# Sixteen of a hybrid decoder layer's 24 gate blocks as pairs of seven half-size products, behind the gMLP units

## The chip, the core and the metric

The kernel runs on one core of a Trainium2 chip. The core has a matrix engine (PE), a vector engine (DVE), a scalar engine (ACT), GpSimd (POOL), a sync engine (SP) that here only issues loads, on-chip memory (SBUF), accumulation banks (PSUM) and DMA queues to DRAM. Each engine works through its own list of instructions in order; semaphores hold an instruction until what it needs is done. The metric is the device time in microseconds (us), the median of three runs. The profile is a trace of one execution.

## The reference

One layer over 1024 tokens of 1024 channels. The normed rows feed one input projection; three mixers (A gMLP, B RG-LRU, C SSD) work on parts of it. Each mixer's output goes through a branch matrix and is weighted by a sigmoid gate that is itself a 1024-column block of the projection. A feed-forward part follows.

```python
hn = rms_norm(h, norm_mix_g[l])
proj = jnp.einsum('bsd,de->bse', hn, w_in[l])
za, zb, zc, xbc, dt_raw, g_raw = jnp.split(proj, SPLIT_POINTS, axis=-1)
ya = gmlp_mixer(za, ...); yb = rg_lru_mixer(zb, ...); yc = ssd_mixer(zc, xbc, dt_raw, ...)
gates = jax.nn.sigmoid(g_raw.reshape(bsz, seq, N_BRANCHES, D_MODEL) + b_gate[l])
merged = (gates[:, :, 0] * jnp.einsum('bse,ed->bsd', ya, w_branch_a[l])
          + gates[:, :, 1] * jnp.einsum('bse,ed->bsd', yb, w_branch_b[l])
          + gates[:, :, 2] * jnp.einsum('bse,ed->bsd', yc, w_branch_c[l]))
h = h + jnp.einsum('bsd,de->bse', merged, w_out[l])
hn = rms_norm(h, norm_mlp_g[l])
up = jax.nn.relu(jnp.einsum('bsd,df->bsf', hn, w_mlp_up[l]))
h = h + jnp.einsum('bsf,fd->bsd', up * up, w_mlp_down[l])
```

## The kernel before

**Tiling.** Channels lie on the 128 partitions, tokens along the row. A float32 operand is split into a rounded high part (ACT, L131) and the rest as a low part (DVE, or POOL for every third weight, L132). A product of two split operands takes three matmuls: high by high, high by low, low by high. A *unit* is 128 output columns of a projection for all 1024 tokens: 8 slices of the inner dimension times 3 parts times 2 token halves, 48 matmuls of 128x512 into one PSUM tile `ps` (`product`, L492 to L498). `run` (L500) takes units from a queue. It first brings the weights of the next units in (`wtile`: load into one of two `raw` buffers, split into the six-buffer pool `w`), then multiplies, then runs the unit's `post`, then `step`, which advances every pending generator by one stage. The compiler's scheduler then sets the order on each engine; code inside `tc.manual_schedule()` keeps the order in which it is written.

**Stages.** First come the norm and the V blocks of gMLP. Then four *rounds* follow (L817 to L823). In each, `ssd_units` queues six units, `lru_units` two units per head for two heads, and gate units of branches 1 and 0 stand between and behind them: one after the SSD units, one after the first head, two after the second (none in the last round). The stages of a mixer (`ssd_stages`: `s1_` to `s4_` for two token halves; `stages` of `lru_units`) run beside later units. Stage `s4_` begins with a matmul of ones by a sum of squares (L683); that sum is a POOL addition (L678) of two squares by ACT (L677) of what `s3_` makes last on DVE (L675). Behind the rounds come the eight gMLP units, each with a Gelu of two ACT and two DVE operations in `post` and a mixing of 16 small matmuls (L788) one unit later, with the last two gate units of branch 0; then the eight gate units of branch 2, whose results stay in SBUF (`keep_gate`), with the rows of `yc` loaded and split beside them (`load_next`, L873, through the two `raw` buffers); then 24 branch units, c, b and a, each of which multiplies its product by (1 + tanh) of the gate (L881 to L885). Then come the output projection (L914 to L945; its PSUM banks come free when x rows loaded on ACT's queue, L938, are added), and the feed-forward part.

**The seven-product scheme** already stands in the feed-forward part: a 2x2 block product with seven half-size products (Strassen's, in Winograd's form) instead of eight. `Weights` (L1007) loads two column blocks and makes the sums of quarters S1 to S4; `seventh` (L958) is one such product, 12 matmuls of 128x512; `Super` (L1050) runs p1 to p7 of it.

**Pools.** `act` has 15 tiles of 128x1024 and ends, with `half`, `lruw` and `const`, before the branches, where `act2` with 27 tiles opens. `mainps` holds two `ps` tiles, `auxps` four half-size tiles.

Of the kernel before, what the change touches and what calls it, by code (L numbers as in the profile page):

```python
# [16 lines left out]
P = 128  # L17
# [19 lines left out]
def trunk_kernel(ctx: ExitStack, tc: tile.TileContext, x, norm_mix_g, w_in, b_gate, gmlp_ln_g, gmlp_ln_b,  # L37
# [20 lines left out]
    xp = normed.enter_context(tc.tile_pool(name="xn", bufs=16, side="right"))  # L58
    mixers = ExitStack()
    halfp = mixers.enter_context(tc.tile_pool(name="half", bufs=16))  # L60
    pools = [mixers.enter_context(tc.tile_pool(name="act", bufs=15))]
# [401 lines left out]

    def wtile(src, n=[0]):
# [55 lines left out]
    gd = [dram.tile([KD, P, T], F32, name=f"g{b}_d") for b in range(2)]  # L520
# [259 lines left out]
    def gmlp_unit(g):  # L780
        def stages(u2):
            yield
# [19 lines left out]
    def gate_unit(br, e, kept=None):  # L802
        def post(ps):
            t = act()
            actv(t, ps, AF.Tanh, scale=0.5, bias=vh[:, BG + br * 8 + e:BG + br * 8 + e + 1])
            if kept:
                kept(t)
            else:
                nc.gpsimd.dma_start(out=gd[br][e], in_=t)
        unit_in(C_G + br * D + e * P, post)  # L810

    gates = [(br, e) for br in (1, 0) for e in range(8)]
# [31 lines left out]
    merged = []  # L844

    def keep_gate(t):
        merged.append(t)
        for k in range(2 * len(merged) - 2, min(2 * len(merged), KD)):
            load_next("c", k)

    for e in range(KD):
        gate_unit(2, e, keep_gate)
    ahead(AHEAD)
    mixers.close()
    pools[0] = ctx.enter_context(tc.tile_pool(name="act2", bufs=27, reuse_waits="tile"))
    late = []

    def act3(shape=(P, T), dt=F32):
        return late[0].tile(list(shape), dt, tag="act3", name=nm("b"))


    def load_y(b, k):
        raw = rawp.tile([P, T], F32, tag="raw", name=nm("raw"))
        nc.sync.dma_start(out=raw, in_=yd[b][k])
        new = act3 if b == "b" else act
# [12 lines left out]
    def branch_unit(b, br, w, e, nxt):  # L878
        def post(ps):
            if b == "c":  # L880
                stt(out=merged[e], in0=merged[e], scalar=1.0, in1=ps, op0=ALU.add, op1=ALU.mult)  # L881
            else:
                t = act()
                nc.scalar.dma_start(out=t, in_=gd[br][e])
                stt(out=t, in0=t, scalar=1.0, in1=ps, op0=ALU.add, op1=ALU.mult)  # L885
# [13 lines left out]
    run()  # L899
    normed.close()  # L900
    late.append(ctx.enter_context(tc.tile_pool(name="act3", bufs=16, side="right", reuse_waits="tile")))
# [44 lines left out]

    sub = ALU.subtract  # L950

    def w4(shape=(P, T), dt=F32):
        return wp.tile(list(shape), dt, tag="w", name=nm("wt"))

    def r4(shape=(P, T), dt=F32):
        return rawp.tile(list(shape), dt, tag="raw", name=nm("rt"))

    def seventh(ps, lhs, rhs, new):  # L958

        n = 0  # L960
        for kk in range(4):
            for l, r in ((0, 0), (0, 1), (1, 0)):
                mm(ps, lhs[l][kk], rhs[r][kk], start=(new and n == 0), stop=(n == 11), skip_group_check=not new)  # L963
                n += 1
# [41 lines left out]

    class Weights:  # L1007


        def __init__(self, src, col, new):  # L1010
            self.new = new
            self.a, self.b = r4((P, KD, P)), act((P, KD, P))
            for t, c0 in ((self.a, col), (self.b, col + P)):
                nc.sync.dma_start(out=t, in_=src[:, c0:c0 + P].rearrange("(k p) e -> p k e", p=P))
            self.op = {}

        def both(self, names, t):
            hi, lo = self.new((P, KD, P), F32R), self.new((P, KD, P), F32R)
            split(hi, lo, t)
            for i, n in enumerate(names):  # L1020
                self.op[n] = [[p[:, 4 * i + kk, :] for kk in range(4)] for p in (hi, lo)]

        def cast1(self):
            self.both(("A11", "A12"), self.a)

        def sums1(self):
            self.s12, self.s34 = act((P, KD, P)), act((P, KD, P))
            tt(out=self.s12[:, 0:4], in0=self.b[:, 0:4], in1=self.b[:, 4:8], op=ALU.add)
            tt(out=self.s34[:, 0:4], in0=self.a[:, 0:4], in1=self.b[:, 0:4], op=sub)

        def sums2(self):
            tt(out=self.s12[:, 4:8], in0=self.s12[:, 0:4], in1=self.a[:, 0:4], op=sub)
            tt(out=self.s34[:, 4:8], in0=self.a[:, 4:8], in1=self.s12[:, 4:8], op=sub)

        def cast12(self):
            self.both(("S1", "S2"), self.s12)

        def cast34(self):
            self.both(("S3", "S4"), self.s34)

        def cast22(self):
            t = act((P, KD, P), F32R)
            split(t[:, 0:4], t[:, 4:8], self.b[:, 4:8])
# [416 lines left out]
```

## Time and profile before

| what | value |
|---|---|
| median of three runs (2030.2 to 2032.55) | 2030.78 us |
| time of the profiled execution | 2033.04 us |
| span of its trace | 2031.3 us |
| mean granted PE clock | 0.991 |
| the four rounds | 127.5 to about 815 us |
| gMLP units, the last two gates of branch 0, the gates of branch 2 | about 815 to 1026 us |
| branch units | to 1287 us |
| output projection, feed-forward part | 1287 to 2031 us |

How to read it: a view of groups gives, for one line of the kernel, engine and shape, how many instructions there were, their busy time and the mean length of one, and what the engine waited for ahead of them. A timeline row is start, length, engine, line, operation, output <- inputs; in brackets stands how long the engine was idle just before and what ended that. A table of windows gives each engine's busy time in a stretch, the granted PE clock (1.00 is full speed), the DMA share and GB/s. PE rows overlap, since matmuls are pipelined; the distance of starts is what one costs.

### The profile page before, as it was taken

The numbers are of one execution on the slowest core, as the hardware profiler recorded it, in microseconds if no ns is written. First come the engines' busy times: TensorE is split into PE (matmuls) and PEld (weight loads), VectorE is DVE, ScalarE is ACT, GpSimd is POOL, SyncE is SP. The second block draws the span as 40 slices with busy tenths as digits, with TensorE's granted clock in tenths as the row PEclk, the third lists the DMA queues.
The fourth block names the chain that finished last, engine by engine and source line by source line (L and its number), as shares of the span: only waits on it lengthen the run. The fifth ranks groups of instructions, "written<-read, shape, count | busy, mean of one in ns | idle before, by whom it ended". The sixth has DMA issues, their size and how long they took to land.

```text
span 2031.3 us, 23733 instructions
## 1 busy us (share of the span) xinstructions
PE 1985.2 (98%) x9300; PEld 1658.2 (82%) x9300; DVE 1196.5 (59%) x1819; ACT 788.4 (39%) x1081; POOL 348.7 (17%) x362
## 2 busy tenths in 40 slices
PE   7999999999999999999999999999899999999996
PEld 7998888888888888888888888887688887888885
DVE  5597774684677468532123224436756657787787
ACT  6422452354245225422221212246555555243243
POOL 4012141222124213431000320000111111000000
PEclk9999999999999999999999999999999999999998
DMA  4224322522422433433333442421444448644532
GB/s 156 76 105 86 89 82 68 113 76 83 96 76 85 95 86 73 127 122 104 114 104 106 148 133 82 165 83 63 155 149 147 161 140 302 211 131 138 187 107 91
DMA packets 202212, 239.38 MB, mean 118 GB/s; under 512 B 11140, under 2 KB 148564, under 8 KB 202100
## 3 DMA queue, kind: packets, MB, share of 16 engines
q1 hardware_dynamic: 175636, 144.91, 24.1%
q0 software_dynamic: 21680, 75.64, 11.6%
q10 hardware_dynamic: 4784, 17.31, 2.4%
q8 instruction: 73, 1.20, 0.3%
q14 instruction: 39, 0.32, 0.1%
HBM read 174.78 MB, written 63.05 MB: 117 GB/s over the span
## 4 chain that ended last, share of the span: by engine, by line
PE 87%; DVE 5%; ACT 4%; issue 2%; POOL 1%; ACTq 0%; POOLq 0%; DVEq 0%
PE ps L497 49%; PE aux L963 26%; PE aux L256 4%; PE aux L932 3%; PE aux L748 1%; ACT a L992 1%; PE aux L788 1%; PE aux L645 1%; DVE rsq_q L110 1%; PE aux L665 1%; PE aux L669 1%; PE aux L683 0%; ACT a L131 0%; DVE b L132 0%; ACT a L970 0%
## 5 line engine op out<-in xcount | busy, mean ns | idle before, releaser
L497 PE MATMUL ps<-xn,wh 128*128 128x512 f32 x2304 | 624.5, 392 | 0.0
L497 PEld LDWEIGHTS ps<-xn,wh 128*128 128x128 f32 x2304 | 430.9, 188 | 93.0 <-issue 4.5
L497 PE MATMUL ps<-xn,wl 128*128 128x512 f32 x1152 | 354.9, 389 | 0.0
L131 ACT ACTIVATE wh<-raw 128x1024 fp32r<-128x1024 f32 x96 | 101.6, 1059 | 394.5 <-PE ps L497 321.2
L497 PEld LDWEIGHTS ps<-xn,wl 128*128 128x128 f32 x1152 | 216.2, 188 | 45.2
L963 PE MATMUL aux<-a,b 128*128 128x512 f32 x864 | 197.3, 389 | 0.0
L963 PEld LDWEIGHTS aux<-a,b 128*128 128x128 f32 x864 | 162.2, 188 | 33.6
L132 DVE TENSOR_TENSOR wl<-raw,wh 128x1024 fp32r<-128x1024 f32 x64 | 81.4, 1271 | 180.9 <-ACT wh L131 179.0
L132 POOL TENSOR_TENSOR wl<-raw,wh 128x1024 fp32r<-128x1024 f32 x32 | 76.8, 2401 | 547.5 <-ACT wh L131 520.9
L963 PE MATMUL aux<-b,wt 128*128 128x512 f32 x672 | 156.9, 389 | 0.0
L963 PEld LDWEIGHTS aux<-b,wt 128*128 128x128 f32 x672 | 126.1, 188 | 26.2
L497 PE MATMUL ps<-a,wh 128*128 128x512 f32 x512 | 136.8, 389 | 0.0
L497 PEld LDWEIGHTS ps<-a,wh 128*128 128x128 f32 x512 | 96.1, 188 | 20.0
L963 PE MATMUL aux<-b,b 128*128 128x512 f32 x480 | 110.6, 389 | 0.0
L1212 DVE TENSOR_TENSOR a<-aux,a 128x512 f32<-128x512 f32 x112 | 76.9, 687 | 50.5 <-PE aux L963 50.5
L963 PEld LDWEIGHTS aux<-b,b 128*128 128x128 f32 x480 | 90.1, 188 | 18.7
L131 ACT ACTIVATE b<-wt 128x1024 fp32r<-128x1024 f32 x60 | 61.9, 1054 | 70.2 <-DMA wt<-u_d 63.9
L963 PE MATMUL aux<-a,wt 128*128 128x512 f32 x336 | 80.3, 396 | 3.4 <-ACT a L1089 3.4
L497 PE MATMUL ps<-a,wl 128*128 128x512 f32 x256 | 78.8, 389 | 0.0
L963 PEld LDWEIGHTS aux<-a,wt 128*128 128x128 f32 x336 | 64.1, 191 | 17.7 <-ACT a L1089 4.2
L517 DVE SCALAR_TENSOR_TENSOR a<-ps,scw,a 128x1023 f32<-128x1023 f32 (+2 forms) x48 | 61.4, 1279 | 25.5 <-ACT a L515 24.5
L1064 POOL DMA_DIRECT2D u_d<-a x48 | 34.6, 721 | 226.2 <-DVE a L1112 177.5
(296 smaller groups left out, 2949.9 us busy)
## 6 DMA issues: line engine op xcount, KB each, us to landing
raw<-in_w_in_dram SPq DMA_DIRECT2D x72, 512.0 KB
wt<-u_d SPq DMA_DIRECT2D x54, 512.0 KB
u_d<-a POOLq DMA_DIRECT2D x48, 512.0 KB, 5.1
rt<-in_w_mlp_up_dram SPq DMA_DIRECT2D x17, 512.0 KB
a<-acs_d POOLq DMA_DIRECT2D x32, 256.0 KB, 6.9
g_d<-a POOLq DMA_DIRECT2D x16, 512.0 KB, 5.1
a<-g_d ACTq DMA_DIRECT2D x16, 512.0 KB
a<-in_w_mlp_down_dram SPq DMA_DIRECT2D x16, 512.0 KB
```

What stands on the lines that cost most here:

```text
L110: stt(out=q, in0=r, scalar=nh, in1=r, op0=ALU.mult, op1=ALU.mult)
L131: actv(dst_hi, src, AF.Copy)
L132: (eng or nc.vector).tensor_tensor(out=dst_lo, in0=src, in1=dst_hi.bitcast(F32), op=ALU.subtract)
L256: mm(ps[:, :nt], X.tok(a, k, c), wk[k][w], start=(k == 0 and i == 0), stop=(k == KD - 1 and i == 2))
L497: mm(ps[:, hsl(h)], w[wi][:, k, :], a.rhs(ai, k, h), start=(n == 0), stop=(n == 3 * KD - 1))
L517: stt(out=dst[:, j:], in0=ps[:, :T - j], scalar=taps[3 - j], in1=dst[:, j:], op0=ALU.mult, op1=ALU.add)
L645: mm(st[:, cc * 256:cc * 256 + 256], Bt[:, 2 * q + cc, :], xw[q][:, cc].rearrange("p h d -> p (h d)"), start=True, stop=True)
L665: mm(yo[:, tok(i)], pv[c // 2][:, c % 2, j * P:(j + 1) * P], Cf[:, tok(c)], start=True, stop=True)
L932: mm(ps, M.tok(a, k, c), wo[nb][k][w], start=(k == 0 and a + w == 0), stop=(k == KD - 1 and a == 1))
L963: mm(ps, lhs[l][kk], rhs[r][kk], start=(new and n == 0), stop=(n == 11), skip_group_check=not new)
L1064: nc.gpsimd.dma_start(out=u_d[i:i + 2, self.s].rearrange("f p t -> p f t"), in_=t.rearrange("p (f t) -> p f t", f=2))
L1212: tt(out=h, in0=ps, in1=h, op=ALU.add)
```

## The change

The gates of branches 0 and 2 (16 blocks of 128 columns) become eight *pairs*. A pair is a 256-column block, split into quarters by output columns and inner dimension, against the normed rows X, split into quarters by inner dimension and token half: seven products of 12 matmuls each (`GatePair`), where two gate units had 96. The sums of quarters of X (T1, T2, T4 in new tiles; T3 in place of the quarter of the first inner half and second token half) are made by `x_forms`, a generator that starts beside gMLP unit 0; the first pair's weights are prepared beside units 6 and 7 (`first_pair`). The pairs run behind the gMLP units in a manual schedule. For them `mainps` is closed and a pool of four half-size PSUM tiles (`gateps`) opened; behind them it is closed and `mainps2` opened. All gates go out to DRAM and come back through ACT's queue in `branch_unit`. In the rounds only the eight gates of branch 1 are left, one after the SSD units and one after the second head. `load_next("c", k)` moves to the last pair (k = 0 to 2) and behind it. `act` lives on until the end of the branches; `act1` (12 tiles) takes the place of `half`, `lruw` and `const`; `act2` opens behind the branches. `sub`, `w4`, `r4`, `seventh` and `Weights` are moved up unchanged.

```diff
-def gate_unit(br, e, kept=None): ...
-gates = [(br, e) for br in (1, 0) for e in range(8)]
+gates = [(1, e) for e in range(8)]
 for r in range(4):
     ssd_units(r)
     some_gates(1)
     lru_units(2 * r)
+    lru_units(2 * r + 1)
     some_gates(1)
-    lru_units(2 * r + 1)
-    some_gates(2 if r < 3 else 0)
 for g in range(8):
     gmlp_unit(g)
-some_gates(2)
...
+def x_forms():
...
+    for kp in range(2):
...
+        d, e = act((P, 4, 2, P)), act((P, 4, 2, P))
+        tt(out=d, in0=quarter(0, 0, 1), in1=quarter(0, 0, 0), op=sub)
+        tt(out=e, in0=quarter(1, 0, 1), in1=quarter(1, 0, 0), op=sub)
+        tt(out=d, in0=d, in1=e, op=ALU.add)
+        in_halves("T1", d)
+        yield
...
+    for kp in range(2):
+        split(X.tile(0, 1, kp), X.tile(1, 1, kp), third[kp])
...
+class GatePair:
...
+    def p1(self):
+        self.b1 = gps.tile([P, HF], F32, tag="gps", name=nm("gps"))
+        self.mul(self.b1, "A11", "B11", True)
+        self.o0 = act()
+        actv(self.o0[:, hsl(0)], self.b1, AF.Copy)
+    def p2(self):
+        b0 = aux()
+        self.mul(b0, "A12", "B21", True)
+        tt(out=self.o0[:, hsl(0)], in0=b0, in1=self.o0[:, hsl(0)], op=ALU.add)
...
+    def p7(self):
+        self.mul(self.b1, "S3", "T3", False)
+        tt(out=self.o1[:, hsl(1)], in0=self.b1, in1=self.o1[:, hsl(1)], op=ALU.add)
+        self.gate(self.o0[:, hsl(1)], self.o0[:, hsl(1)], 0)
+        nc.gpsimd.dma_start(out=gd[self.br][self.e], in_=self.o0)
+    def p4(self):
+        self.mul(self.b1, "A22", "T4", False)
+        self.gate(self.o1[:, hsl(0)], self.b1, 1)
+        self.gate(self.o1[:, hsl(1)], self.o1[:, hsl(1)], 1)
+        nc.gpsimd.dma_start(out=gd[self.br][self.e + 1], in_=self.o1)
...
-for e in range(KD):
-    gate_unit(2, e, keep_gate)
+wide.close()
+gps = gatep.enter_context(tc.tile_pool(name="gateps", bufs=4, space=bass.MemoryType.PSUM))
...
     def post(ps):
+        t = act1() if b == "c" and e < 4 else act()
+        nc.scalar.dma_start(out=t, in_=gd[br][e])
+        stt(out=t, in0=t, scalar=1.0, in1=ps, op0=ALU.add, op1=ALU.mult)
...
+with tc.manual_schedule():
+    z.w.cast22()
+    while z:
+        nxt = GatePair(*pairs.pop(0)) if pairs else None
+        z.p1()
+        z.w.cast34()
+        if prev:
+            prev.p4()
+        z.p2()
+        if nxt:
+            nxt.w.cast1()
+        z.p5()
...
+        z.p6()
...
+        z.p3()
...
+        z.p7()
+        if not nxt:
+            load_next("c", 2)
+        prev, z = z, nxt
+    prev.p4()
...
+load_next("c", 3)
+mixers.close()
+more.append(mixers.enter_context(tc.tile_pool(name="act1", bufs=12, reuse_waits="tile")))
+for k in range(4, KD):
+    load_next("c", k)
```

**PE at the end of a round (round 1).** Before, `ps_3823` is the x unit of the round's second head and `ps_3912` its gate-input unit; `aux_3892` is the matmul of ones that opens `s4_` of the second token half:

```order
L497 MATMUL ps_3823<-xn_248,wh_3587 128x512
L497 MATMUL ps_3823<-xn_563,wh_3587 128x512
L497 MATMUL ps_3823<-xn_241,wl_3588 128x512
L497 MATMUL ps_3823<-xn_557,wl_3588 128x512
L683 MATMUL aux_3892<-h_3794,ones 128x512
L497 MATMUL ps_3912<-xn_226,wh_3720 128x512
L497 MATMUL ps_3912<-xn_539,wh_3720 128x512
```

Now `ps_3725` is the second head's gate-input unit and `ps_3847` the round's last gate unit; `aux_3780` is the same matmul of ones:

```order
L556 MATMUL ps_3725<-xn_241,wl_3473 128x512
L556 MATMUL ps_3725<-xn_557,wl_3473 128x512
L556 MATMUL ps_3847<-xn_226,wh_3605 128x512
L556 MATMUL ps_3847<-xn_539,wh_3605 128x512
L556 MATMUL ps_3847<-xn_232,wh_3605 128x512
L742 MATMUL aux_3780<-h_3696,ones 128x512
L807 MATMUL aux_3795<-h_3670,lw_3666 128x512
L807 MATMUL aux_3795<-h_3671,lw_3666 128x512
```

The matmul of ones stood behind the first unit that follows `s3_`'s matmuls; it still does, but three matmuls later, and 45 matmuls of `ps_3847` are now queued behind it.

**DVE at the same place.** Before: L758 and L763 belong to the first head's scan, L672 to L675 to `s3_` (the second L675 is what the squares wait for), L132 and L517 to the next weights and to the second head's convolution:

```order
L758 SCALAR_TENSOR_TENSOR h_3698<-h_3706 128x512
L672 TENSOR_TENSOR h_3646<-aux_3776,h_3646 128x512
L673 TENSOR_TENSOR h_3646<-aux_3777,h_3646 128x512
L672 TENSOR_TENSOR h_3649<-aux_3796,h_3649 128x512
L763 SCALAR_TENSOR_TENSOR a_3671<-h_3684,h_3682 128x512
L674 SCALAR_TENSOR_TENSOR h_3646<-a_3063,dcol,h_3646 128x512
L763 SCALAR_TENSOR_TENSOR a_3671<-h_3706,a_3671,h_3704 128x512
L675 TENSOR_TENSOR a_3196<-h_3646,a_3196 128x512
L673 TENSOR_TENSOR h_3649<-aux_3797,h_3649 128x512
L674 SCALAR_TENSOR_TENSOR h_3649<-a_3126,dcol,h_3649 128x512
L675 TENSOR_TENSOR a_3305<-h_3649,a_3305 128x512
L132 TENSOR_TENSOR wl_3909<-raw_3906,wh_3908 128x1024
```

Now (L731 to L734 are the old L672 to L675, L822 the scan, L576 the convolution, L133 the splits), from the scan on:

```order
L822 SCALAR_TENSOR_TENSOR a_3556<-h_3591,a_3556,h_3589 128x512
L576 SCALAR_TENSOR_TENSOR a_3658<-ps_3609,va,a_3658 128x1023
L734 TENSOR_TENSOR a_3081<-h_3531,a_3081 128x512
L576 SCALAR_TENSOR_TENSOR a_3658<-ps_3609,va,a_3658 128x1022
L731 TENSOR_TENSOR h_3534<-aux_3698,h_3534 128x512
L576 SCALAR_TENSOR_TENSOR a_3658<-ps_3609,va,a_3658 128x1021
L732 TENSOR_TENSOR h_3534<-aux_3699,h_3534 128x512
L133 TENSOR_TENSOR wl_3722<-raw_3719,wh_3721 128x1024
L133 TENSOR_TENSOR h_3671<-a_3658,h_3670 128x512
L733 SCALAR_TENSOR_TENSOR h_3534<-a_3011,dcol,h_3534 128x512
L133 TENSOR_TENSOR h_3675<-a_3658,h_3674 128x512
L734 TENSOR_TENSOR a_3190<-h_3534,a_3190 128x512
```

Three convolution steps, a weight split and two half-size splits have moved ahead of the second L734 (the old L675).

**SP and DVE at the end of the gates.** SP before: two rows of `yc` between the weights of one gate unit and the next (the first 7 of such rows):

```order
L466 DMA raw_7257<-in_w_in_dram 128x8x128
L864 DMA raw_7314<-yc_d 128x1024
L864 DMA raw_7320<-yc_d 128x1024
L466 DMA raw_7326<-in_w_in_dram 128x8x128
L864 DMA raw_7383<-yc_d 128x1024
L864 DMA raw_7389<-yc_d 128x1024
L466 DMA raw_7395<-in_w_in_dram 128x8x128
```

SP now, from the last pair's weights (`rt_7611`, `a_7612`) to the weights of the first three branch units:

```order
L490 DMA rt_7611<-in_w_in_dram 128x8x128
L490 DMA a_7612<-in_w_in_dram 128x8x128
L525 DMA raw_7801<-in_w_branch_c_dram 128x8x128
L1027 DMA raw_7820<-yc_d 128x1024
L1027 DMA raw_7839<-yc_d 128x1024
L1027 DMA raw_7860<-yc_d 128x1024
L1027 DMA raw_7886<-yc_d 128x1024
L1027 DMA raw_7898<-yc_d 128x1024
L1027 DMA raw_7904<-yc_d 128x1024
L1027 DMA raw_7910<-yc_d 128x1024
L1027 DMA raw_7916<-yc_d 128x1024
L525 DMA raw_7926<-in_w_branch_c_dram 128x8x128
```

DVE now, in the last pair: L937, L952 and L956 are the additions of p2, p3 and p7, L133 the low parts of the rows of `yc`, L1045 the first branch unit's gate product:

```order
L937 TENSOR_TENSOR a_7750<-aux_7771,a_7750 128x512
L133 TENSOR_TENSOR a_7823<-raw_7820,a_7822 128x1024
L952 TENSOR_TENSOR a_7750<-aux_7785,a_7750 128x512
L133 TENSOR_TENSOR a_7842<-raw_7839,a_7841 128x1024
L956 TENSOR_TENSOR a_7798<-gps_7737,a_7798 128x512
L133 TENSOR_TENSOR a_7863<-raw_7860,a_7862 128x1024
```

The loads of `yc`, which lay beside four gate units, now follow one another through the two `raw` buffers; and the low part of the second row of `yc` stands ahead of p7's addition, which p4 waits for, since p4 adds into the same bank.

More of the change, by code (lines that the diff above doesn't have):

```diff
@@ L781, in stages @@
         def stages(u2):
+            if g == 0:
+                later(x_forms())
+            elif g == 5:
+                later(first_pair())
             yield
@@ L805, in post @@
             actv(t, ps, AF.Tanh, scale=0.5, bias=vh[:, BG + br * 8 + e:BG + br * 8 + e + 1])
[L806 to L809, printed above, removed]
+            nc.gpsimd.dma_start(out=gd[br][e], in_=t)
         unit_in(C_G + br * D + e * P, post)
[L812 removed]
+    XF = {n: [[X.rhs(part, 4 * kh + kk, th) for kk in range(4)] for part in range(2)]
+          for n, kh, th in (("B11", 0, 0), ("B21", 1, 0), ("B22", 1, 1), ("T3", 0, 1))}
@@ L813, in some_gates, with first_pair @@
+    pairs = [(br, e) for br in (0, 2) for e in range(0, KD, 2)]
+    cur = []
+    def first_pair():
+        z = GatePair(*pairs.pop(0))
+        cur.append(z)
+        yield
+        z.w.cast1()
+        z.w.sums1()
+        yield
+        z.w.sums2()
+        z.w.cast12()
+    gates = [(1, e) for e in range(8)]
     def some_gates(n):
@@ L843, in trunk_kernel, with act1 @@
         step()
[L844 to L849, printed above, removed]
-    for e in range(KD):
-        gate_unit(2, e, keep_gate)
[L853 to L856, printed above, removed]
+    wide.close()
+    gatep = ExitStack()
+    gps = gatep.enter_context(tc.tile_pool(name="gateps", bufs=4, space=bass.MemoryType.PSUM))
+    late, more = [], []
     def act3(shape=(P, T), dt=F32):
         return late[0].tile(list(shape), dt, tag="act3", name=nm("b"))
+    def act1(shape=(P, T), dt=F32):
+        return more[0].tile(list(shape), dt, tag="act1", name=nm("c"))
     def load_y(b, k):
@@ L945, in trunk_kernel @@
             tt(out=h[:, hsl(0)], in0=pss[i], in1=h[:, hsl(0)], op=ALU.add)
[L950 to L964, printed above, removed]
     Nf = {}
@@ L1005, in quad @@
         return [Nf[th, 2 * kh], Nf[th, 2 * kh + 1]]
[L1007 to L1043, printed above, removed]
-            self.op["A22"] = [[t[:, 4 * p + kk, :] for kk in range(4)] for p in range(2)]
     def square_relu(c):
```

131 lines of the change are left out of this document (120 added, 11 removed).

## The prediction

> **What bounds the kernel now.** I read the page first, then the chain of waits in order of time, then windows by stage (columns: window; length; busy PE, PE loads, DVE, ACT, POOL; PE clock; DMA).
>
> ```profile
> PE 1985.2 (98%) x9300; PEld 1658.2 (82%) x9300; DVE 1196.5 (59%) x1819; ACT 788.4 (39%) x1081; POOL 348.7 (17%) x362
> 127.54 32.66 PE ps L497 x144
> 928.19 359.06 PE ps L497 x1584
> 1449.43 241.28 PE aux L963 x1056
> 363.00:540.00 177.00, 176.36 (x854) 145.93 (x853) 116.58 (x169) 70.83 (x81) 41.62 (x37) 1.00 0.32 85
> 816.00:939.00 123.00, 123.00 (x609) 104.22 (x608) 48.65 (x51) 36.75 (x41) 47.85 (x37) 1.00 0.41 124
> 1024.00:1074.00 50.00, 50.00 (x222) 41.41 (x221) 14.69 (x12) 11.39 (x11) 4.81 (x2) 1.00 0.36 109
> 1452.00:1690.00 238.00, 238.00 (x1047) 196.99 (x1046) 143.42 (x189) 127.86 (x188) 33.14 (x49) 1.00 0.47 163
> ```
>
> PE bounds nearly every stage. The chain runs on it for 359.06 us without a break through 1584 matmuls: 0.2267 us each, 10.88 us for a unit of 48. In a round (363 to 540) PE is idle 0.6 us of 177; around the gates and the branches it is never idle. So a matmul removed is worth its 0.2267 us, and any wait put onto PE costs its whole length.
>
> **What is removed.** Sixteen gate units are 768 matmuls; eight pairs of seven products of 12 are 672. 96 x 0.2267 = **-21.8 us**. The same scheme runs between 1452 and 1690 us at 241.28 / 1056 = 0.2285 us a matmul with no idle PE, with DVE at 60% and ACT at 54%. A gate pair asks for less: on DVE three low parts, a half one, four half sums and three additions, on ACT three and a half splits, three copies and four tanh, which by the rows below is about 9.2 us of DVE and 8 of ACT in 84 x 0.2267 = 19.0 us. So inside the stage the pairs keep PE's rate, and I cost this work at nothing; were that cover gone it would be 9.2 us a pair.
>
> ```profile
> L132 DVE TENSOR_TENSOR wt<-a,wt 128x1024 fp32r<-128x1024 f32 x26 | 31.9, 1226 | 8.3 <-ACT wt L131 8.3
> L1033 DVE TENSOR_TENSOR a<-rt,a 128x512 f32<-128x512 f32 x13 | 9.0, 692 | 0.5
> L131 ACT ACTIVATE wt<-a 128x1024 fp32r<-128x1024 f32 x26 | 27.5, 1058 | 2.5 <-DVE a L1032 2.1
> ```
>
> The sums of X are 24 full and 8 half operations of DVE, 24 x 1.226 + 8 x 0.692 = 35 us, and the first pair's preparation 5: about 40 us beside gMLP, where DVE has 48.65 us of work in 123 (816 to 939). They fit, with a DVE at some 85%; only their end shows, below. The eight extra stores and loads of gates cost POOL and ACT an issue each, beside products.
>
> **What is added in the rounds.** This is the largest term. Round 1 now, at the matmul of ones that opens `s4_` of the second token half:
>
> ```profile
> 435.42 1.19 PE L497 MATMUL ps<-xn,wh 128*128 128x512 f32 x4
> 447.02 1.13 PE L683 MATMUL aux<-h,ones 128*128 128x512 f32 x2 [0.43 <-POOL h L678]
> 436.70 2.29 DVE L763 TENSOR_TENSOR_SCAN a<-h,h 128x512 f32<-128x512 f32 x1 [1.50 <-POOL h L762]
> 444.25 0.69 DVE L675 TENSOR_TENSOR a<-h,a 128x512 f32<-128x512 f32 x1
> 445.69 1.28 POOL L678 TENSOR_TENSOR h<-h,h 128x512 f32<-128x512 f32 x1 [0.97 <-ACT h L677]
> 447.27 1.23 DVE L132 TENSOR_TENSOR wl<-raw,wh 128x1024 fp32r<-128x1024 f32 x1 [2.33 <-ACT wh L131]
> 448.41 3.91 DVE L517 SCALAR_TENSOR_TENSOR a<-ps,va,a 128x1023 f32<-128x1023 f32 x3
> 453.08 1.29 DVE L132 TENSOR_TENSOR h<-a,h 128x512 fp32r<-128x512 f32 x2 [0.76 <-ACT h L131]
> 432.25 2.57 POOL L132 TENSOR_TENSOR wl<-raw,wh 128x1024 fp32r<-128x1024 f32 x1 [0.92 <-PE aux L665]
> ```
>
> The chain L675 (444.25), square, POOL sum (445.69), L683 (447.02) ends just as the unit that began at 435.42 does; PE waits 0.43. In the new order the gate unit between the two heads is gone, so the second head's convolution is ready earlier, and DVE runs its three steps, a weight split and two half splits ahead of that last L675. By the distance of starts (1.14 for the split, 1.2 for a step between other work, 0.6 for a half split) that is 3.6 + 1.14 + 1.2 = 5.9 us, so the matmul of ones would be ready at 452.9. PE gets there after one unit and three matmuls, 435.42 + 10.88 + 0.68 = 447.0, and waits; 45 matmuls of the gate unit and the next head's are queued behind. Against that stands DVE's idle time ahead of the scan, 1.50 us there, due to POOL's weight split at 432.25, which the new order has elsewhere, and some 0.6 us of smaller gaps. The extra wait is between 5.9 - 2.1 - 0.4 = 3.4 and 5.5 us; I take **3.7**, near the low end, as POOL is free there. The end of every round has this order: 4 x 3.7 = **+14.8 us**.
>
> What a wait does to the clock (windows; then two groups of matmuls with the wait ahead of them):
>
> ```profile
> 1428.00:1432.00 4.00, 2.91 (x13) 2.41 (x14) 3.79 (x5) 3.54 (x6) 0.00 (x0) 1.00 0.00 0
> 1448.00:1452.00 4.00, 2.57 (x8) 2.04 (x9) 3.04 (x5) 1.87 (x4) 0.57 (x1) 0.83 1.05 305
> 1452.00:1456.00 4.00, 4.00 (x15) 3.21 (x14) 2.51 (x3) 2.08 (x3) 0.00 (x0) 0.74 1.04 383
> 1429.09 3.02 PE L963 MATMUL aux<-a,a 128*128 128x512 f32 x12 [1.67 <-ACT a L1093]
> 1449.43 5.76 PE L963 MATMUL aux<-a,wt 128*128 128x512 f32 x17 [2.59 <-ACT a L1089]
> ```
>
> After 1.67 us of idle PE the clock stayed at 1.00; after 2.59 us it fell, and 8 us at 0.83 and 0.74 lost 4 x 0.17 + 4 x 0.26 = 1.7 us. Waits of 4 us lie beyond that, but where the drop falls is not steady; between 0 and 4 x 1.7 I take two of four: **+3.4 us**.
>
> The Trainium skill ("TensorE: Matmul & The Clock Gate", section on the HAM clock gate) says that an idle window of about 3.4 us halves the clock, and that a busy one restores it. By that rule all four waits could drop it, an estimate of 4 x 1.7 = 6.8 us in place of 3.4, and a sum of 2047. The trace differs in that 2.59 us were enough.
>
> **What is added where the pairs begin.** p1's PSUM pool opens only when the last gMLP unit's Gelu has left `mainps`:
>
> ```profile
> 913.73 1.78 PE aux L788 x16
> 914.33 1.01 ACT L234 ACTIVATE a<-ps 128x1024 f32<-128x1024 f32 x1
> 917.94 1.22 DVE L237 SCALAR_TENSOR_TENSOR a<-a,ps 128x1024 f32<-128x1024 f32 x1 [1.13 <-ACT a L236]
> 919.08 1.40 DVE L789 SCALAR_TENSOR_TENSOR a<-aux,vh,bs 128x512 f32<-128x512 f32 x2
> ```
>
> A unit ends at 913.73, its Gelu at 919.16, 5.4 us later (about 4.9 without the weight split ahead of the square). PE has two mixings for that time, 3.6 us: p1 waits 1.3. p2 needs a bank that a mixing leaves on DVE behind T4's low part and two half sums, 4.9 + 1.2 + 1.4 + 0.7 = 8.2, when p1 ends at 7.6: 0.6. p5 needs the low part of S1 and S2, behind six more operations (5.8 us, at 14.0), when p2 has ended at 10.9 and two matmuls can go ahead: 2.6. Together 4.5; POOL's products slow DVE now and then, so **+5 us** (3.5 to 8).
>
> **What is added where they end.** All rows of `yc` now pass the two `raw` buffers in one go. Their cycle (SP's issue, split on ACT, low part on DVE, and one on POOL):
>
> ```profile
> 960.08 0.32 SPq L864 DMA_DIRECT2D raw<-yc_d  x1
> 963.57 1.06 ACT L131 ACTIVATE a<-raw 128x1024 fp32r<-128x1024 f32 x1 [0.62 <-DMA raw<-yc_d]
> 964.72 1.23 DVE L132 TENSOR_TENSOR a<-raw,a 128x1024 fp32r<-128x1024 f32 x1 [0.52 <-ACT a L131]
> 969.38 2.39 POOL L132 TENSOR_TENSOR wl<-raw,wh 128x1024 fp32r<-128x1024 f32 x1 [27.77 <-ACT wh L131]
> ```
>
> Issue to the end of the low part is 964.72 + 1.23 - 960.08 = 5.9 us. Count from the end of the last p7. ACT splits branch weight 0 only after p5's copy, at about -5.7; POOL's low part, 2.4, frees the buffer at -3.2. Row 1 of `yc` follows, its low part done at 2.8, and only then DVE makes p7's addition: p4 waits 3.5. On the same buffer rows 3, 5 and 7 follow at 8.7, 14.6 and 20.5. The first branch unit needs row 7 last, ends at 21.4, and the second, whose weights come next on the other buffer, at about 34.5. Without waits it would end at 2.7 + 21.8 = 24.5: **+10 us** (7 to 14, since nine gate loads share the DMA). Before, four gate units hid these loads.
>
> **What is added behind the branches.** `act2` now opens there, so one split of w_out more falls behind the last unit.
>
> ```profile
> 1301.29 1.06 ACT L131 ACTIVATE a<-raw 128x1024 fp32r<-128x1024 f32 x1 [3.63 <-DMA raw<-in_w_out_dram]
> 1301.30 6.17 ACTq L938 DMA_DIRECT2D a<-in_x_dram  x8
> 1307.20 0.69 DVE L945 TENSOR_TENSOR a<-aux,a 128x512 f32<-128x512 f32 x1 [3.60 <-DMA a<-in_x_dram]
> ```
>
> The x loads are issued with the last such split, 14.0 us after the branches' end (928.19 + 359.06), and the first addition ends 20.6 after it; the bank is wanted at 96 x 0.2267 = 21.8. Half a cycle of 5.9 later, the addition ends at 23.6: **+1.9 us** (0 to 4).
>
> **Sum.** 2033.0 - 21.8 + 14.8 + 3.4 + 5 + 10 + 1.9 = 2046.3 us for the profiled execution, which lay 2.3 us above the median: **2044 us**.
>
> **The rivals.**
> - *The matmul of ones comes in time* (chance 0.20): the scheduler set it three matmuls into a unit, so by its costs DVE is done by then. No round waits: -21.8 + 16.9 = -4.9, 2025.9 us on the median's scale; with the junctions at their low ends (3.5 + 7 + 0) -11.3, 2019.5. For it speaks that L683 waited only 0.43 before; against it, that scan and POOL sum took 2.29 and 1.28 us.
> - *All is covered* (0.06): the junctions too are hidden, 2009 us, faster. Against it stand two `raw` buffers and 5.9 us a cycle.
> - *The waits are at their upper ends* (0.14): 4 x 5.5 in the rounds and the clock drops every time: -21.8 + 22 + 6.8 + 16.9 = +23.9, 2054.7 us. It decides if POOL's work still holds the scan back.
> - The forecast (0.60).
>
> **Range and chances.** A measurement tells 0.2%, 4.1 us, from no change. The range takes in the first rival down to its low end and the third: 2019 to 2056. Faster: the second rival and most of the first, 0.06 + 0.14 = 0.20; same: the rest of the first and a part of the forecast, whose low bounds (-21.8 + 4 x 3.4 + 3.5 + 7 + 0) come to +2.3, 0.06 + 0.08 = 0.14; slower 0.66.
>
> **What would show it.** Right: PE idle about 4 us ahead of L742, from POOL L737, once at each round's end; idle PE at the first p1, p2 and p5, none from the second pair to the last p7; p4 waiting for DVE L956; the first branch unit waiting for splits of `yc`. Wrong: rounds 21.8 us shorter than 177 with PE still full, or a branch unit that starts right behind p4.

## The result and the profile after

| | before | after |
|---|---|---|
| median | 2031.62 us (the 3 runs above and a fourth) | 2059.84 us (4 runs, 2057.14 to 2061.29) |
| profiled execution, span | 2033.04, 2031.3 us | 2061.29, 2059.5 us |
| mean granted PE clock | 0.991 | 0.983 |

The ratio is 1.0138, with a 95% interval of 1.0120 to 1.0156: the changed kernel is slower by 28 us. The forecast was slower by 13, and 2059.84 lies above the range (2019 to 2056).

The first part of the page of after: busy time, share and instructions.

```profile
PE 1981.5 (96%) x9204; PEld 1650.2 (80%) x9204; DVE 1305.1 (63%) x1929; ACT 814.7 (40%) x1141; POOL 342.4 (17%) x364
```

PE has the 96 matmuls less that were expected, which are worth 21.8 us, but its busy time fell by only 3.7 us: those left took longer, at a mean granted clock of 0.983 for 0.991. The rest of the loss is idle PE. It is lost at four places.

**The rounds.** First the chain of waits of before, then that of after, at the long stretch of matmuls in rounds 2 and 3 (start, length, what; rounds are counted from 0):

```profile
463.82 74.12 PE ps L497 x327
640.95 74.12 PE ps L497 x327
```

```profile
446.57 59.62 PE ps L556 x263
606.90 59.62 PE ps L556 x263
```

A round took 177.13 us and takes 160.33. Two units fewer are worth 96 x 0.2267 = 21.76, so 155.37 was to be had: each of these rounds loses 4.96 us. The timeline of after at the end of round 1, DVE, POOL and PE:

```profile
428.51 1.27 DVE L576 SCALAR_TENSOR_TENSOR a<-ps,va,a 128x1021 f32<-128x1021 f32 x1
430.29 1.21 DVE L133 TENSOR_TENSOR wl<-raw,wh 128x1024 fp32r<-128x1024 f32 x1
432.69 0.68 DVE L133 TENSOR_TENSOR h<-a,h 128x512 fp32r<-128x512 f32 x1
433.29 0.68 DVE L734 TENSOR_TENSOR a<-h,a 128x512 f32<-128x512 f32 x1
434.78 1.26 POOL L737 TENSOR_TENSOR h<-h,h 128x512 f32<-128x512 f32 x1 [7.66 <-ACT h L736]
436.09 1.12 PE L742 MATMUL aux<-h,ones 128*128 128x512 f32 x2 [3.82 <-POOL h L737]
```

The last L734 starts at 433.29, behind the convolution, the weight split and the half splits; POOL had been idle for 7.66 us and PE waits 3.82. Then the windows (columns as in the prediction):

```profile
436.00:438.00 2.00, 1.91 (x5) 1.29 (x6) 2.00 (x2) 1.28 (x3) 0.04 (x1) 0.82 0.00 0
438.00:440.00 2.00, 2.00 (x6) 1.52 (x6) 2.00 (x2) 1.99 (x2) 0.00 (x0) 0.50 0.83 217
440.00:442.00 2.00, 2.00 (x9) 1.59 (x8) 2.00 (x2) 2.00 (x4) 0.00 (x0) 0.83 0.16 45
```

The clock falls behind the wait: 2 x (0.18 + 0.50 + 0.17) = 1.7 us more. The other three rounds wait as long (3.81 to 3.83 us). In round 0 the clock falls for longer: from the matmul of ones at 274.75 to the long stretch behind it, at 286.24, PE takes 11.49 us, 1.0 more than the 10.48 from 436.09 to 446.57.

**The start of the pairs.** PE in the timeline of after:

```profile
870.13 3.73 PE L851 MATMUL aux<-wT,a 128*128 128x128 f32 x32
876.20 4.36 PE L480 MATMUL gps<-xn,wt 128*128 128x512 f32 x12 [2.34 <-DVE a L238]
884.88 0.73 PE L480 MATMUL aux<-h,wt 128*128 128x512 f32 x2 [1.31 <-ACT wt L132]
886.67 2.60 PE L480 MATMUL aux<-h,wt 128*128 128x512 f32 x10 [1.05 <-DVE wt L133]
1028.21 2.88 PE L480 MATMUL gps<-xn,wt 128*128 128x512 f32 x12
```

The mixings end at 873.7. The last p7 stands 648 matmuls behind the first p1's start (8 x 84, less the last p7 and p4); 873.7 + 648 x 0.2267 = 1020.6, and it starts at 1028.21: the start loses 7.6 us. From the second pair on there is no wait.

**The end of the pairs.** The chain of waits of after, from the first row of `yc` that waits for a buffer:

```profile
1027.64 3.45 DMA raw<-yc_d
1032.29 1.24 DVE a L133
1033.54 4.67 DMA raw<-yc_d
1039.41 1.24 DVE a L133
1040.66 7.94 DMA raw<-yc_d
1049.72 1.24 DVE c L133
1050.97 6.58 DMA raw<-yc_d
1058.68 1.22 PE ps L556 x2
1064.46 249.63 PE ps L556 x1100
```

One `raw` buffer does this: load, split, free, load, for rows 1, 3, 5 and 7. PE hangs on it till 1058.68. What PE itself shows (timeline), and two windows:

```profile
1034.17 4.60 PE L480 MATMUL gps<-a,a 128*128 128x512 f32 x12 [3.07 <-DVE a L956]
1040.01 1.20 PE L556 MATMUL ps<-a,wh 128*128 128x512 f32 x4 [1.23 <-ACT a L926]
1058.68 2.48 PE L556 MATMUL ps<-c,wh 128*128 128x512 f32 x4 [3.60 <-ACT c L132]
```

```profile
1044.00:1048.00 4.00, 3.10 (x14) 2.25 (x12) 0.00 (x0) 0.00 (x0) 0.00 (x0) 1.00 0.93 365
1052.00:1056.00 4.00, 3.08 (x8) 1.86 (x6) 0.14 (x1) 0.00 (x0) 0.00 (x0) 0.61 0.97 344
```

p7, p4 and 24 branch units are 1176 matmuls, 266.6 us; from 1028.21 they would end at 1294.8 and end at 1314.1: 19.3 us are lost. In the windows ACT, DVE and POOL stand still while the DMA is at 93 and 97%.

**Behind the branches** the span goes on for 2059.5 - 1314.1 = 745.4 us, where it was 2031.3 - 1287.25 = 744.05: 1.4 us more. PE waits as long for the first addition of a row of x (L1156):

```profile
1337.24 4.38 PE L1143 MATMUL aux<-wb,b 128*128 128x512 f32 x18 [1.40 <-DVE a L1156]
```

### The profile page after: what moved, and what is told of

Same layout as the page of the kernel before. It is cut to its first block, busy times and chain, and to the rows that moved or that the text cites. A ratio compares the mean times of both kernels' runs of the same rounds, so it can differ in the third digit from the quotient of the medians.

```text
span 2059.5 us, 23757 instructions
## 1 busy us (share of the span) xinstructions
PE 1981.5 (96%) x9204; PEld 1650.2 (80%) x9204; DVE 1305.1 (63%) x1929; ACT 814.7 (40%) x1141; POOL 342.4 (17%) x364
## 4 chain that ended last, share of the span: by engine, by line
PE 80%; DVE 8%; ACT 5%; issue 4%; DMA 2%; POOL 1%; ACTq 0%; DVEq 0%; POOLq 0%
PE ps L556 38%; PE aux L480 28%; PE aux L257 4%; PE gps L480 3%; PE aux L1143 2%; PE aux L807 1%; DMA raw<-yc_d 1%; DVE a L133 1%; ACT a L1184 1%; PE aux L704 1%; DVE rsq_q L111 1%; ACT a L132 1%; PE aux L742 0%; POOL h L821 0%; PE rps L161 0%
## 5 line engine op out<-in xcount | busy, mean ns | idle before, releaser
L556 PE MATMUL ps<-xn,wh 128*128 128x512 f32 x1792 | 486.7, 392 | 0.0
L556 PEld LDWEIGHTS ps<-xn,wh 128*128 128x128 f32 x1792 | 335.5, 188 | 71.9 <-issue 3.3
L556 PE MATMUL ps<-xn,wl 128*128 128x512 f32 x896 | 275.9, 389 | 0.0
L556 PEld LDWEIGHTS ps<-xn,wl 128*128 128x128 f32 x896 | 168.4, 188 | 35.3
L132 ACT ACTIVATE wh<-raw 128x1024 fp32r<-128x1024 f32 x80 | 84.5, 1057 | 263.8 <-PE ps L556 227.1
L133 POOL TENSOR_TENSOR wl<-raw,wh 128x1024 fp32r<-128x1024 f32 x26 | 66.1, 2542 | 457.6 <-ACT wh L132 457.6
L133 DVE TENSOR_TENSOR wl<-raw,wh 128x1024 fp32r<-128x1024 f32 x54 | 69.0, 1278 | 110.6 <-ACT wh L132 110.6
L132 ACT ACTIVATE b<-wt 128x1024 fp32r<-128x1024 f32 x60 | 61.9, 1053 | 69.8 <-DMA wt<-u_d 53.5
L133 DVE TENSOR_TENSOR wt<-a,wt 128x1024 fp32r<-128x1024 f32 x44 | 53.9, 1225 | 48.4 <-ACT wt L132 48.4
L556 PE MATMUL ps<-c,wh 128*128 128x512 f32 x256 | 71.0, 399 | 6.8 <-ACT c L132 6.2
L133 DVE TENSOR_TENSOR a<-a,a 128x1024 fp32r<-128x1024 f32 (+1 forms) x55 | 54.4, 997 | 33.8 <-ACT a L132 33.7
L1045 DVE SCALAR_TENSOR_TENSOR a<-a,ps 128x1024 f32<-128x1024 f32 x20 | 24.4, 1221 | 76.8 <-PE ps L556 57.5
L133 DVE TENSOR_TENSOR b<-wt,b 128x1024 fp32r<-128x1024 f32 x60 | 72.9, 1216 | 0.0
```

The costliest lines, as they stand in the source:

```text
L132: actv(dst_hi, src, AF.Copy)
L133: (eng or nc.vector).tensor_tensor(out=dst_lo, in0=src, in1=dst_hi.bitcast(F32), op=ALU.subtract)
L556: mm(ps[:, hsl(h)], w[wi][:, k, :], a.rhs(ai, k, h), start=(n == 0), stop=(n == 3 * KD - 1))
```

## The experiments

All of them start from the changed kernel, unless stated; 2059.84 us is what they are compared with. The measured losses of start and end are counted as above.

**The order in the rounds put back.**

```diff
         lru_units(2 * r)
+        some_gates(1)
         lru_units(2 * r + 1)
-        some_gates(1)
```

> Only the order in the rounds is put back: the second gate unit of a round stands between the two heads again; pairs, start and end stay as changed. Theory (DVE runs the second head's convolution and splits ahead of the last addition that the matmul of ones needs, because no gate unit lies between the heads): the 3.8 us of idle PE ahead of L742 falls to under 0.6 in each of the four rounds, the clock stays at 1.00 there, a round takes 155 to 156 us in place of 160.3, and the time falls by 4 x 5 = 20 us, to about 2040. Rival (two gate units fewer leave DVE, busy 113 us of 160, too little cover, and the wait comes up at another place of the round): a round stays at 158 us or more, the time at 2052 to 2060.

Measured 2037.76 us (ratio to before 1.0033, interval 1.0022 to 1.0043): 22.1 us faster. The group of the matmul of ones over the whole run, the matmul of round 1 with the weight split and the convolution of DVE, and the chain of waits at the same place of rounds 2 and 3:

```profile
L742 PE MATMUL aux<-h,ones 128*128 128x512 f32 x16 | 8.9, 637 | 2.0 <-POOL h L737 1.2 <-ACT a L677 0.8
424.66 1.12 PE L742 MATMUL aux<-h,ones 128*128 128x512 f32 x2 [0.30 <-POOL h L737]
425.03 1.22 DVE L133 TENSOR_TENSOR wl<-raw,wh 128x1024 fp32r<-128x1024 f32 x1 [2.46 <-ACT wh L132]
426.17 3.91 DVE L576 SCALAR_TENSOR_TENSOR a<-ps,va,a 128x1023 f32<-128x1023 f32 x3
```

```profile
439.87 53.95 PE ps L556 x238
595.08 53.95 PE ps L556 x238
```

The split and the convolution stand behind the matmul of ones again. PE waits 1.2 us for POOL in all where it waited 15.3, and a round takes 155.21 us. The theory holds; the rival falls, since this run has as few gate units in its rounds as the changed kernel.

**The same order alone, in the kernel before.** The mirror of it, without pairs.

```diff
         lru_units(2 * r)
-        some_gates(1)
         lru_units(2 * r + 1)
-        some_gates(2 if r < 3 else 0)
+        some_gates(3 if r < 3 else 1)
```

> The kernel before, with one thing changed: the gate unit between the two heads of a round goes behind the second head, so that the heads follow each other as in the changed kernel; no pairs. Theory (this order alone makes the wait at the matmul of ones): PE waits 3.8 us ahead of L683 at the end of each round and loses some 1.5 us to the clock behind it, 4 x 5.2 = 21 us, time about 2052. Rival (it takes the shorter rounds, with two gate units fewer): the time stays within 4 us of before, 2028 to 2035.

Measured 2054.81 us, 23.4 slower than before (ratio 1.0113, 1.0099 to 1.0127). The group over the run:

```profile
L683 PE MATMUL aux<-h,ones 128*128 128x512 f32 x16 | 11.5, 809 | 17.1 <-POOL h L678 16.3 <-ACT a L618 0.8
```

16.3 us of waiting for POOL, with four gate units in each of the first three rounds. That two heads follow each other is enough; the number of gate units is not what decides.

**No gate loads for branch c** (its products are copied, not weighted: the gates of branch c are left out).

```diff
-            nc.scalar.dma_start(out=t, in_=gd[br][e])
-            stt(out=t, in0=t, scalar=1.0, in1=ps, op0=ALU.add, op1=ALU.mult)
+            if b == "c":
+                actv(t, ps, AF.Copy)
+            else:
+                nc.scalar.dma_start(out=t, in_=gd[br][e])
+                stt(out=t, in0=t, scalar=1.0, in1=ps, op0=ALU.add, op1=ALU.mult)
```

> The eight branch units of c no longer load their gates and copy the product instead of weighting it (left out: gates of branch c). Theory (the gate loads on ACT's queue share the DMA with the rows of yc and the branch weights, which is why a raw buffer's cycle took 7.1 to 10.3 us in place of 5.9): the cycle falls to 6 to 7 us, the last row is there some 6 us earlier, the waits between the last p7 and the second branch unit fall from 19.3 to about 13 us, time about 2053. Rival (the two raw buffers and a load's own latency set the cycle): waits unchanged within 2 us, time 2058 to 2060.

Measured 2051.48 us, 8.4 less. The loads in its chain of waits:

```profile
1024.00 3.42 DMA raw<-yc_d
1029.86 4.83 DMA raw<-yc_d
1039.27 5.36 DMA raw<-yc_d
```

No load takes 7.94 us any more, and the end loses 12.2 us in place of 19.3. So the gate loads cost some 7 us here by sharing the DMA with rows that pass two buffers. The other 12 stay without them; p4 still waits 3.04 us for p7's addition.

**The rows of `yc` past the buffers.** Every row is loaded into the tile of its low part and split in place; the pool `act1` opens at the last pair's p6, with rows 2 to 7 issued there.

```diff
     def load_y(b, k):
+        new = act3 if b == "b" else (act if k < 4 else act1)
+        if b == "c":
+            l_, h_ = new(dt=F32R), new(dt=F32R)
+            nc.sync.dma_start(out=l_.bitcast(F32), in_=yd[b][k])
+            return h_, l_
         raw = rawp.tile([P, T], F32, tag="raw", name=nm("raw"))
...
+    def split_y(k):
+        split(Y["c"].p[0][k], Y["c"].p[1][k], Y["c"].p[1][k].bitcast(F32))
...
                 ahead(1)
+                load_next("c", 0)
+                load_next("c", 1)
             z.p6()
...
-                load_next("c", 0)
+                mixers.close()
+                more.append(mixers.enter_context(tc.tile_pool(name="act1", bufs=12, reuse_waits="tile")))
+                for k in range(2, KD):
+                    load_next("c", k)
+                split_y(0)
...
-            else:
-                load_next("c", 1)
             z.p7()
             if not nxt:
-                load_next("c", 2)
+                split_y(1)
             prev, z = z, nxt
         prev.p4()
+        for k in range(2, KD):
+            split_y(k)
```

> The rows of yc no longer pass the raw buffers: each is loaded straight into the tile of its low part, all eight loads are issued by the last pair's p6, and the split of row 1 stands behind p7's addition on DVE. The gate loads stay. Theory (the two raw buffers in turn, and DVE's order at p7, make the 19.3 us): p4 no longer waits for DVE, all rows are split within some 10 us of the last p7, the 19.3 us fall to 3 to 6 (the new PSUM pool still waits for p4's tanh), time 2044 to 2047. Rival (the DMA is the bound there: 8 rows, 9 gates and 3 weights of 0.52 MB at some 345 GB/s are 30 us however they are issued): the waits fall by less than 6 us, time 2054 to 2058.

Measured 2042.52 us, 17.3 less, a little better than the theory's 2044. The chain of waits at that place:

```profile
1031.88 3.07 PE gps L480 x12
1034.97 0.70 ACT a L926
1035.71 34.34 PE ps L556 x150
```

p4 follows p7 with 0.8 us of waiting, the first branch unit follows p4's tanh, and from then on PE is not idle: the end loses 2.4 us. The gate loads are all still there and now hide beside matmuls, so the DMA isn't the bound by its sum; rows that wait for a buffer are. The edit also takes row 1's split from ahead of p7's addition and starts the loads earlier; the next run has the first of these alone, the second was not tried alone.

**Only the order of p7's addition and row 1.**

```diff
-            else:
-                load_next("c", 1)
             z.p7()
             if not nxt:
+                load_next("c", 1)
                 load_next("c", 2)
```

> The changed kernel with the second row of yc loaded and split behind p7's addition in place of ahead of it. Theory (the arrival of the last rows through the two buffers sets the end, and p4's wait for the addition only lies inside it): p4's 3.1 us wait is gone, the waits ahead of the branch unit's products grow by as much, time 2058 to 2061. Rival (p4's wait adds to the rest): 3 to 5 us less, 2055 to 2057.

Measured 2056.28 us (2051.76 to 2057.8), 3.6 less: the rival's numbers, but little beyond the noise (ratio to before 1.0104 to 1.0132, where the changed kernel has 1.0120 to 1.0156). In the profiled execution, its fastest, p4 waits 0.78 us for the addition and the end loses 13.5 us in place of 19.3. There the theory, that p4's wait lies inside that for the last rows, fell. The loads of the chain took 4.25, 5.45 and 4.91 us where they had taken 4.67, 7.94 and 6.58; why the later rows come sooner was not tried.

**Two plain units ahead of seven pairs.**

```diff
-    pairs = [(br, e) for br in (0, 2) for e in range(0, KD, 2)]
+    pairs = [(br, e) for br in (0, 2) for e in range(0, KD, 2)][1:]
...
-    gates = [(1, e) for e in range(8)]
+    gates = [(1, e) for e in range(8)] + [(0, 0), (0, 1)]
...
         gmlp_unit(g)
+    some_gates(2)
```

> One pair fewer: blocks 0 and 1 of branch 0 are plain units again (2 x 48 matmuls for 84, +2.7 us) and stand behind the gMLP units, ahead of the pairs. Theory (the start of the pairs loses 7.6 us because nothing on PE covers the last Gelu, the closing of the pool and the end of DVE's sums): idle PE and slow clock there fall to under 2 us, the time falls by 7.6 - 1 - 2.7 = about 4 us, to 2056. Rival (DVE has too much to do in the whole stretch, 70 of 80 us, and the sums and preparations move along with the units): the waits ahead of p1 to p5 stay, time 2060 to 2064.

Measured 2053.66 us, 6.2 less, though 12 matmuls (2.7 us) more. The first p1:

```profile
893.68 2.60 PE L480 MATMUL gps<-xn,wt 128*128 128x512 f32 x10 [1.20 <-ACT a L868]
```

p1 waits 1.2 us for the last tanh, and p2 to p5 for nothing. The start loses 1.5 us. The theory holds: 7.6 - 1.5 - 2.7 = 3.4 us come from the start. The rest of the 6.2 does not: the profiled execution reaches its first mixing at 790.88 us, where the changed kernel's had it at 794.05, and nothing was edited ahead of it.

**What at the start is late: two attempts.** gMLP's product moved from POOL to DVE, and (apart from it) the first pair prepared one gMLP unit earlier:

```diff
-            nc.gpsimd.tensor_tensor(out=y, in0=y, in1=u2, op=ALU.mult)
+            tt(out=y, in0=y, in1=u2, op=ALU.mult)
```

```diff
-            elif g == 5:
+            elif g == 4:
                 later(first_pair())
```

> The changed kernel with gMLP's product L854 on DVE instead of POOL (eight operations of 1.2 us more on DVE). Theory (each product on POOL holds up one DVE operation of two operands for 2.2 us, eight of them between 790 and 895 us, and so DVE is late for p1 to p5): no DVE operation there takes over 2 us any more, DVE gains 1 us for each, the 7.6 us lost at the start of the pairs fall to 3 to 5, time 2055 to 2057. Rival (the long DVE rows have another cause): DVE has 10 us more to do, the start loses 9 to 12 us, time 2061 to 2064.

> The changed kernel with the first pair's preparation started one gMLP unit earlier, so that its sums L504 to L509 stand ahead of the last gMLP unit's Gelu on DVE and not behind it; the amount of DVE work is the same. Theory (DVE, full from 852 to 892 us and with 7 us of idle time between 832 and 852, does the first pair's sums too late for p5): the waits at p1 to p5 fall from 7.6 to 3 to 5 us, time 2055 to 2057. Rival (it is the whole of DVE's work that is late, or the last Gelu and the PSUM pool): the start loses 7 us or more still, time 2059 to 2061.

Measured 2059.55 and 2061.96 us: neither gains; the start loses 7.9 and 9.1 us, counted as above. The first, PE in the timeline at p5:

```profile
881.03 0.73 PE L480 MATMUL aux<-h,wt 128*128 128x512 f32 x2 [3.07 <-ACT wt L132]
```

The long DVE rows are gone there as the theory had it (below), yet p5 waits 3.07 us for the high part of S1 and S2, which ACT splits behind DVE's sum L508; in the scheduler's new order that sum stands behind the product L854 and the last sums of X. The second, DVE and PE:

```profile
877.45 1.23 DVE L133 TENSOR_TENSOR a<-a,a 128x1024 fp32r<-128x1024 f32 x1 [3.97 <-DMA ya_d<-a]
890.27 2.11 PE L480 MATMUL aux<-xn,wt 128*128 128x512 f32 x8 [1.96 <-DVE wt L133]
```

The sums are early now, but DVE stands for 3.97 us until a row of `ya` is stored and its tile of `act` is free. Both theories fell as to the time. That a unit on PE covers the start is shown; which of Gelu, DVE's queue and the 15 tiles of `act` would have to go for a start without cover stays open.

**Together.** Old order in the rounds, rows past the buffers, two plain units ahead of seven pairs:

> The three edits together: the old order in the rounds (alone -22.1 us), the rows of yc straight into their tiles (alone -17.3) and two plain units ahead of seven pairs (alone -6.2). Theory (three separate places on PE's path): they add up, 2059.8 - 45.6 = 2014 us, between 2011 and 2018, that is 0.7 to 0.9% faster than the kernel before. Rival (waits taken from one place come up behind another, as DVE and the DMA get to each stage sooner): 2020 to 2030, no faster than before by more than 0.4%.

Measured 2015.64 us, ratio 0.9928 (0.9914 to 0.9941): faster than before by 16 us. The three gains add up to 45.6, and 44.2 came. Three variants with all eight pairs: the preparation one unit earlier in place of plain units; one gate unit of branch 1 moved from the last round to behind the gMLP units; two of them, from the last two rounds.

> Old order in the rounds, rows of yc straight into their tiles, the first pair prepared one unit earlier; all eight pairs. Theory (the parts add up): 2059.8 - 22.1 - 17.3 - 3 = 2017 us, between 2015 and 2020, by the start's remaining wait. Rival (with the rounds unhindered DVE is further behind at the start, as the sums begin with the first gMLP unit in either case): 2020 to 2024.

> Old order in the rounds, rows of yc straight into their tiles, all eight pairs, and the gate unit behind the SSD units of the last round moved to behind the gMLP units. Theory (one unit of 10.9 us covers the start as two did, and the pair given up for them was worth 2.7 us; the last round's SSD stages do without that unit): 2015.6 - 2.7 = 2013 us, between 2011 and 2015. Rival (in the last round the stages of the SSD heads are then late for PE): a wait of 4 to 8 us there, 2017 to 2021.

> As the run with one gate unit moved from the last round to behind the gMLP units, with a second one moved from the third round: two plain units of branch 1 ahead of all eight pairs. Theory (two units cover the start, where one left 4 us of idle PE and slow clock; the rounds do without both): 2017.0 - 4 = 2013 us, 2011 to 2015. Rival (the round without its first gate unit makes the SSD stages late, as the last round's, with no SSD units after it, did not): a wait of 4 us or more in the third round, 2016 to 2020.

Measured 2022.16, 2016.98 and 2015.25 us (ratio of the last 0.9917, 0.9904 to 0.9931). The first loses 10.7 us at the start, and its time is the rival's. In the second, p1 waits 2.21 us for the moved unit's tanh and the start loses 4.1: one unit covers less than two, and the theory's 2013 was missed. In the third the start loses 1.5, as with two units above, and PE waits once at the start of the last round (605.95), 1.47 us for a convolution, and nowhere in the round before it; its time lies just above the theory's 2011 to 2015 and can't be told from that of the kernel with seven pairs.

## Why the prediction was right and wrong

By the terms of its sum, in us of the profiled execution:

| term | forecast | measured | how |
|---|---|---|---|
| matmuls removed | -21.8 | -21.8 | 96 fewer in the page |
| rounds, waits and clock | +18.2 | +21.3 | first mixing at 837.5, now 794.1: six units (65.3) fewer, 0.6 lost before the rounds |
| start of the pairs | +5 | +7.6 | above |
| end of the pairs | +10 | +19.3 | above |
| behind the branches | +1.9 | +1.4 | above |
| sum | +13.3 | +28.4 with the 0.6 | 2061.29 - 2033.04 = 28.25 |

- **The matmuls.** Right, and the pairs keep PE's rate from the second on. With the losses of the rounds, the end and the start taken out the change gains: 2015.64 with seven pairs, 2015.25 with eight.
- **The rounds.** The mechanism was right, and so was the size of the waits. PE waits 3.82 us ahead of L742; 3.7 was the forecast for the extra wait, and 15.3 - 1.5 = 13.8 us is that of four rounds, for 14.8. The clock was undersized: it fell in all four rounds, not in two, and 21.3 - 13.8 leaves 7.5 us to it, for 3.4. That is near what the prediction worked out from the Trainium skill ("TensorE: Matmul & The Clock Gate", section on the HAM clock gate), 6.8 us in place of 3.4; all four waits were 3.8 us, above that rule's 3.4, and by that rule the trace agrees here. How often the clock falls is in part luck: six runs have the same rounds and the same waits, and in three of their 24 the clock stayed at 1.00 (last section). The rival that the matmul of ones comes in time is refuted.
- **The start.** The places were right (p1, p5, twice), at 7.6 within the 3.5 to 8 stated. p2 waited for no bank. Not in the sum was that the clock falls there too: the window 878 to 882 has 0.62, which is 4 x 0.38 = 1.5 us.
- **The end** is where the prediction failed, in the term "issue to the end of the low part is 5.9 us". That cycle was read at 960 us, beside a gate unit, where nothing else was being loaded (the DMA was 39% busy from 960 to 964). The three cycles of one buffer took 7.1, 10.3 and 8.9 us (ACT's splits at 1031.20, 1038.32, 1048.63 and 1057.57), 26.4 in place of 17.7, so the last row came 8.7 us later; that is nearly all of the 9.3 us missed. Its load took 6.58 us, the one before 7.94, against 3.5: the gate loads, which the prediction gave up to 4 us, cost 7 by the run without them. The path was right (p4 behind DVE's L956, the first branch unit behind the splits of `yc`); what a load takes on a full DMA was wrong. Smaller misses: the pool `mainps2` opens only behind p4's tanh (1.23), and the clock fell here as well.
- **Behind the branches** the path and the size were right: the first addition ends 23.1 us behind the branches (23.6 was forecast), and the loss is right to half a microsecond.

The sum missed 15 us: 9.3 at the end, 3.1 in the rounds, 2.6 at the start. The rival with all upper ends (2054.7) had 14 for the end, and was still too low: its bound for that one term, too, was worked out from a transfer on a quiet DMA.

## What to carry to other kernels

A unit of independent matmuls between two dependent chains is cover, also when it looks like filler: before it is taken out, look at what the vector engine then runs ahead of the last operation that the next matmul waits for. A transfer's time read where the DMA is idle is no price for a burst: where a change gathers loads, add up everything else that starts in the same stretch, and count the buffers that the loads pass in turn. Loading straight into the tile that will hold the result takes such a ring of buffers off the path.

## What the runs showed of the hardware

A product on POOL holds up DVE for as long as it lasts. The timeline of the changed kernel, POOL and DVE beside gMLP:

```profile
801.00 3.30 POOL L854 TENSOR_TENSOR a<-a,a 128x1024 f32<-128x1024 f32 x1 [16.50 <-DVE a L852]
801.96 3.42 DVE L893 TENSOR_TENSOR a<-xn,xn 128x1024 f32<-128x1024 f32 x1
866.43 2.76 POOL L854 TENSOR_TENSOR a<-a,a 128x1024 f32<-128x1024 f32 x1 [6.18 <-DVE a L852]
866.86 3.42 DVE L133 TENSOR_TENSOR xn<-a,xn 128x1024 fp32r<-128x1024 f32 x1
```

Both DVE operations take 1.22 us elsewhere. Each began while POOL's ran and ended 1.1 us after it (805.38 against 804.30, 870.28 against 869.19); by these ends it stood still until POOL was done, and then did its own work. This happened beside seven of the eight products, and beside the eighth (840.61 to 843.00) DVE started nothing; with the product on DVE one row of DVE there took over 1.6 us, 2.47. The Trainium skill ("SBUF — State Buffer", section "Summary: rules for kernel authors") says the same: the second of the two to issue fully blocks until the first finishes, if DVE has two inputs in SBUF and POOL's operation reads SBUF. The trace agrees, at 1.6 to 2.2 us for each.

The same wait does not always drop the PE clock. The run with gMLP's product on DVE has the rounds of the changed kernel; in its round 1 PE waits 3.81 us ahead of the matmul of ones at 434.66, and then works on at full clock:

```profile
436.00:438.00 2.00, 2.00 (x11) 1.63 (x10) 2.00 (x2) 1.97 (x3) 0.00 (x0) 1.00 0.50 127
```

So it was also in round 1 of the run without the gate loads and in round 3 of the run with the earlier preparation; the other 25 of 28 such waits, in seven runs, were followed by a fall. On the other side the clock fell after idle stretches of 2.1 us and less where several stood close together: in the run with only p7's order changed (first two rows) PE was busy for 6.8 of 8 us, at a clock of 0.67 and 0.55. In the run without the gate loads (last two rows) it stayed at 1.00 with PE busy for 5.1 of 8 us, where no wait was longer than 0.94 us. What decides was not tried.

```profile
1044.00:1048.00 4.00, 2.80 (x6) 1.46 (x6) 1.23 (x1) 1.25 (x2) 0.00 (x0) 0.67 0.96 330
1052.00:1056.00 4.00, 3.96 (x9) 2.32 (x10) 2.00 (x2) 1.06 (x1) 0.00 (x0) 0.55 0.96 292
1044.00:1048.00 4.00, 2.95 (x11) 1.64 (x10) 1.71 (x2) 1.06 (x1) 0.00 (x0) 1.00 0.37 132
1048.00:1052.00 4.00, 2.14 (x7) 0.97 (x6) 1.23 (x1) 1.67 (x2) 0.00 (x0) 1.00 0.54 158
```
